# First layer's remaining modulation vectors: two weight blocks per visit, loaded into the softmax's wide tiles

## The chip, the cores and the metric

The kernel runs on one NeuronCore of a Trainium2 chip. A core has several engines with an instruction queue each: TensorE (PE) multiplies matrices, VectorE (DVE) and ScalarE (ACT) work elementwise, GpSimd (POOL) does a little of both, and SyncE (SP) issues the DMA transfers here. An engine runs its own queue in order and waits on semaphores for the others. The metric is the device time of one execution in microseconds (us), as the median of several runs.

## The reference

A transformer block of two layers, one sequence of 256 tokens (`x`) and a second stream of 256 context tokens (`ctx`), width 1024. Per layer, cut to what matters:

```python
mod = s_c @ w_mod[i] + b_mod[i]              # 6 vectors of 1024: sh1, sc1, gt1, sh2, sc2, gt2
mod_c = s_ctx @ w_mod[i] + b_mod[i]          # the same for the context (layer 1: two of them)
h = modulate(rms_norm(x, g_norm1[i]), sh1, sc1);  hc = the same of ctx
p = h @ w_in[i]                              # keys, queries, values, u, v, gate logits; pc from hc
y_na  = neighbourhood_attention(q_na, k_na, v_na, k_na_c, v_na_c, rpb)   # 8 heads of 64
y_gm  = spatial_gating(gelu(u), gelu(v), ...)
y_mla = dense_attention(q_mla, [k_mla_c, k_mla], [v_mla_c, v_mla])       # 8 heads of 96
mix = merge_branches(y_na, y_gm, y_mla, gates, na_w_o, gm_w_o, mla_w_o, w_out)
x = x + gt1 * mix
x = x + gt2 * squared_relu_mlp(modulate(rms_norm(x), sh2, sc2), w1, w2)
```

In layer 0 the context passes through all of this as well; in layer 1 it only gives keys and values. So layer 0 works on 512 columns (both streams) and layer 1 on 256. The shift and scale `sh1`, `sc1` are needed before anything else; the other four vectors (`gt1`, `sh2`, `sc2`, `gt2`) only after `merge_branches`. These four are the "other modulation vectors" of the title.

## The kernel before, in words

Activations stand transposed: 128 features on the partitions, tokens in the columns. Projections run in the precision of fp32 by splitting each operand in a rounded high part and the rest and adding three multiplications, high by high, high by low and low by high (`mm3`; lines 287, 288 and 289 of the profile). ScalarE makes the high part of a weight block (`wh`, line 115) and VectorE the rest (`wl`, line 116). `gemm_a` projects one chunk of 128 output features: 8 blocks of input features, so 24 multiplications of 512 columns in layer 0.

Weights come through `load` (line 94): a DMA of 512 KB (128 x 1024 fp32) from SyncE's queue into the ring `raw` of three buffers. `last_load` remembers the latest one; `tc.issue_after` orders other transfers behind it.

The order of the work on each engine is set when the program is built: the tile framework takes the operations of all parts and orders them by a simulated time line, within what data, buffers, priorities and `issue_after` allow. On the chip each engine then runs its list in order. So a small edit can move many instructions.

Layer 0 around the change runs like this: projections, then `u` (the loop at line 708, four chunks), the gating step `sg`, the neighbourhood attention (two heads at a time through `soft_pv`), the keys and values of the second attention (`kv`, with the transposes `h_tr`), its queries (`qm`), the second attention (`soft_pv` again, outputs `pvm`), and the merges. `merge(l, b, ...)` computes for branch b the gate logits (`gate`) and the branch's output projection (`z`), chunk by chunk. Multiplications of a merge are spread beside an attention by `paced`: `marks` holds the score multiplications, and each block of a gate or of `z` is released behind one of them. Branch 0 (gating) has its first four chunks beside the neighbourhood attention and the other four between the two attentions; branch 1 and the first gates of branch 2 go beside the second attention; the rest of branch 2 follows unpaced.

`soft_pv` (line 429) does a pair of heads and one stream: the score `S`, its maximum and the exponential `P` (ScalarE, line 448), four transposes `pt` (line 454) into one PSUM buffer, a copy by ScalarE to `PT` (line 456), and the product with the values (`pv`, `pvm`, line 460). `PT` is a wide tile, 128 x 1024 fp32 like a weight block, with two buffers, one for each head of the pair. The FFN's `load(..., extra=True)` uses the same two buffers under the name `rawx`.

The other modulation vectors are made by four generators `mod_group` (line 168), g = 2 to 5, each over the eight 128 x 1024 blocks of its part of `wmod`. Each step of a generator is a *visit*: `load` one block into `raw`, then `mod_cols`, four multiplications of a 128 x 32 operand by 256 columns each (the silu of both conditions, of which two columns hold data), and `yield`. The trace shows a visit as eight records of `mod_ps`, line 137. `bg()` (line 122) takes one step of the first generator that isn't through. It is called in the `u` loop (`bg(2)`, line 710) and in each chunk of each merge (line 478). After the eighth block `mod_finish` copies the sums to `mod_sb`, transposes them (`mod_t`) and adds the bias.

Of the kernel before, what the change touches and what calls it, by code (L numbers as in the profile page):

```python
# [7 lines left out]
F32 = mybir.dt.float32  # L8
# [15 lines left out]
KC = 8  # L24


def hybrid_block_kernel(tc, a, out):
    nc = tc.nc
    act = nc.scalar.activation
    vec = nc.vector  # L30
    mm = nc.tensor.matmul

    from contextlib import ExitStack, nullcontext
    with ExitStack() as es:
# [7 lines left out]
        gp = pool("g")  # L42
# [40 lines left out]
        sS = cp.tile([128, KC, 32], F32, name="sS")  # L83
# [12 lines left out]
        last_load = [None]  # L96

        def load(ap, width=1024, extra=False):
            if extra:
                raw = gp.tile([128, 1024], F32, tag="PT", name="rawx", bufs=2)  # L100
            else:
                raw = wp.tile([128, 1024], F32, tag="raw", name="raw", bufs=3)
            dma = nc.sync.dma_start(out=raw[:, :width], in_=ap)
            if not extra:
                last_load[0] = dma.ins
            return raw
# [15 lines left out]
        def bg(n=1):  # L122
            while n and background:
                try:
                    next(background[0])
                    n -= 1
                except StopIteration:
                    background.pop(0)
# [5 lines left out]
        def mod_cols(ps, raw, off, w, k):  # L134
            for j in range(4):
                o = off + j * w
                mm(ps[32 * j:32 * j + 32, :w], lhsT=sS[:, k, :], rhs=raw[:, o:o + w], start=(k == 0), stop=(k == KC - 1),
                   tile_position=(0, 32 * j))

        def mod_finish(ps, w, dsts, modT, bmod, streams):  # L140

# [25 lines left out]

        def mod_group(l, g, modT, bmod, streams):
            ps = psum("mm", "mod_ps")
            for k in range(KC):  # L170
                raw = load(a["wmod"][l, g - 2, k])
                mod_cols(ps, raw, 0, 256, k)
                yield
            mod_finish(ps, 256, lambda m, i: m[:, 8 * g:8 * g + 8].rearrange("p (j i) -> p j i", i=2)[:, :, i], modT, bmod,
                       streams)

# [297 lines left out]
        def merge(l, b, yH, yL, hH, hL, ymix, T, ns=range(8), pace=None, gated={}):  # L474

            mixH, mixL = [], []
            for n in ns:
                bg()
                if n in gated:
                    th = gated[n]  # L480
                    if n % 2 == 0:
                        zraw = load(a["wo"][l, b, n // 2])
                else:
                    gw = split(load(a["wa"][l, 4 + 8 * b + n]))
                    if n % 2 == 0:
                        zraw = load(a["wo"][l, b, n // 2])
                    gps = psum("mm", "gate")
                    gemm_a(gps, gw, hH, hL, T, pace=pace)
                    th = tmp2("th")
                    act(out=th[:, :T], in_=gps[:, :T], func=AF.Tanh, scale=0.5)  # L490
                zps = psum("mm", "z")
                gemm_a(zps, [split1(zraw[:, (n % 2) * 512:(n % 2) * 512 + 512], 512)], yH, yL, T, pace=pace)
                if b == 0:
                    o = xp.tile([128, NT], F32, tag="ymix", name="ymix", bufs=8)
                    vec.scalar_tensor_tensor(out=o[:, :T], in0=th[:, :T], scalar=1.0, in1=zps[:, :T], op0=ALU.add,
                                             op1=ALU.mult)
                    ymix.append(o)
                else:
                    o = ymix[n]
                    vec.scalar_tensor_tensor(out=th[:, :T], in0=th[:, :T], scalar=1.0, in1=zps[:, :T], op0=ALU.add,  # L500
                                             op1=ALU.mult)
                    vec.tensor_tensor(out=o[:, :T], in0=o[:, :T], in1=th[:, :T], op=ALU.add)
                if b == 2:
                    H, Lo = parts("mix", T)
                    act(out=H[:, :T], in_=o[:, :T], func=AF.Copy, scale=0.5)
                    vec.scalar_tensor_tensor(out=Lo[:, :T], in0=o[:, :T], scalar=0.5, in1=H[:, :T], op0=ALU.mult,
                                             op1=ALU.subtract)
                    mixH.append(H)
                    mixL.append(Lo)
            return mixH, mixL  # L510
# [17 lines left out]
        first, rest = begin_mod(0)  # L528
# [18 lines left out]
        for l in range(L):  # L547
# [22 lines left out]
            with tc.issue_after(last_load[0]):  # L570
                if l == 0:
# [8 lines left out]
                                  in_=a["kqrow"][l:l + 1, :].to_broadcast([128, 64]))  # L580
# [20 lines left out]
            for w in range(2):  # L601
                for t in range(2):
                    vec.tensor_tensor(out=rC[:, w, t, :], in0=ropeC[:, t, :], in1=kqrow[:, w, :], op=ALU.mult)
                    for hf in range(2):
                        o = rS[:, w, t, :].rearrange("p (a b f) -> p a b f", a=2, b=2)[:, :, hf, :]
# [19 lines left out]
            for t in range(4):  # L625
                o = gp.tile([128, 512], F32, tag="v", name="vna", bufs=4)
# [83 lines left out]
                                  op1=ALU.mult)  # L710
            u = []
            for n in range(4):
                bg(2)
                ws = split(load(a["wa"][l, n]))
                ups = psum("mm", "u")
                gemm_a(ups, ws, hH, hL, T)
                o = g2("u", F32)
                act(out=o[:, :T], in_=ups[:, :T], func=AF.Gelu)
                u.append(o)
# [350 lines left out]
```

## Time and profile before

| | |
|---|---|
| median of 3 runs | 1403.13 us (1402.51 to 1403.38) |
| the profiled execution's own time | 1402.83 us |
| its span, first to last instruction | 1400.8 us |
| TensorE busy | 1370.2 us (98%) |
| VectorE, ScalarE, GpSimd busy | 957.4 (68%), 704.7 (50%), 56.9 us (4%) |
| chain that ended last | TensorE 96%, VectorE, DMA and ScalarE 1% each |

The span is what the page's parts divide; the execution's own time has 2.0 us more around it. Busy time of TensorE is modelled for pipelined multiplications: one that is shown as 0.39 us may be followed by the next 0.22 us after its start, so steps are read from start to start, and an idle time in square brackets is what the engine stood still before a row. The name behind the arrow in the brackets is what ended the wait.

### The profile page before, as it was taken

What the parts mean: (1) busy time and instruction counts of PE and PEld (TensorE: products, weight loads), DVE (VectorE), ACT (ScalarE), POOL (GpSimd) and SP (SyncE); (2) the same over time, 40 slices, a digit from 0 to 9 for tenths busy, and PEclk for the clock granted to TensorE, in tenths of its full rate; (3) what the DMA queues carried; (4) which work ended last, traced back from release to release, by engine and by line L of the source; (5) the groups of instructions that cost most, each with busy time, mean ns of one, the idle gap of its engine ahead of it and who ended that gap; (6) DMA issues with size and microseconds to landing.
All of it is one profiled execution on the core that took longest, in us unless ns stands there. A gap on an engine that the chain in (4) does not pass through costs nothing.

```text
span 1400.8 us, 22572 instructions
## 1 busy us (share of the span) xinstructions
PE 1370.2 (98%) x8438; PEld 1161.8 (83%) x8438; DVE 957.4 (68%) x2071; ACT 704.7 (50%) x1440; POOL 56.9 (4%) x35
## 2 busy tenths in 40 slices
PE   6999999999999999999999999999999999999999
PEld 4788767777676789988888888988888878999998
DVE  4666477665563558899766665786787766877775
ACT  3466256443453346623324233566676665656654
POOL 0110000110000000000000000011002100000000
PEclk9999999999999999999999999999999999999999
DMA  9423542234313465665555552443543434566664
GB/s 331 142 84 106 187 150 90 71 105 123 119 46 114 127 195 168 208 202 172 203 205 188 175 197 89 150 137 94 181 136 99 136 91 136 181 181 180 183 183 148
DMA packets 67214, 210.61 MB, mean 150 GB/s; under 512 B 8609, under 2 KB 9633, under 8 KB 67105
## 3 DMA queue, kind: packets, MB, share of 16 engines
q1 hardware_dynamic: 67104, 209.18, 46.6%
q8 instruction: 66, 1.08, 0.3%
q14 instruction: 44, 0.35, 0.1%
HBM read 208.10 MB, written 1.05 MB: 149 GB/s over the span
## 4 chain that ended last, share of the span: by engine, by line
PE 96%; DVE 1%; DMA 1%; ACT 1%; issue 0%; SPq 0%; POOL 0%; ACTq 0%; DVEq 0%
PE o_ps L287 8%; PE o_ps L289 8%; PE o_ps L288 8%; PE f L288 6%; PE f L287 6%; PE f L289 6%; PE gate L287 5%; PE gate L288 5%; PE gate L289 5%; PE b_ps L287 5%; PE b_ps L288 4%; PE b_ps L289 4%; PE pt L454 3%; PE S L417 2%; PE z L287 2%; PE z L289 2%
## 5 line engine op out<-in xcount | busy, mean ns | idle before, releaser
L115 ACT ACTIVATE wh<-raw 128x512 fp32r<-128x512 f32 (+1 forms) x570 | 353.1, 626 | 515.8 <-PE o_ps L288 179.7
L116 DVE TENSOR_TENSOR wl<-raw,wh 128x512 fp32r<-128x512 f32 (+1 forms) x570 | 385.8, 683 | 178.1 <-ACT wh L115 172.7
L289 PE MATMUL f<-hH,wl 128*128 128x258 f32 (+2 forms) x560 | 180.9, 324 | 0.1
L287 PE MATMUL f<-hH,wh 128*128 128x258 f32 (+2 forms) x560 | 180.4, 323 | 0.5 <-ACT wh L115 0.5
L288 PE MATMUL f<-hL,wh 128*128 128x258 f32 (+2 forms) x560 | 180.4, 324 | 0.2 <-DVE hL L277 0.2
L288 PE MATMUL o_ps<-aL,wh 128*128 128x256 f32 (+1 forms) x544 | 176.1, 327 | 0.0
L287 PE MATMUL o_ps<-aH,wh 128*128 128x256 f32 (+1 forms) x544 | 176.0, 328 | 0.0
L289 PE MATMUL o_ps<-aH,wl 128*128 128x256 f32 (+1 forms) x544 | 175.6, 328 | 0.0
L287 PE MATMUL gate<-hH,wh 128*128 128x512 f32 (+1 forms) x384 | 140.5, 366 | 0.0
L289 PE MATMUL gate<-hH,wl 128*128 128x512 f32 (+1 forms) x384 | 130.3, 339 | 0.0
L288 PE MATMUL gate<-hL,wh 128*128 128x512 f32 (+1 forms) x384 | 130.1, 339 | 0.0
L287 PEld LDWEIGHTS f<-hH,wh 128*128 128x128 f32 x560 | 106.0, 190 | 9.1 <-ACT wh L115 0.7
L289 PEld LDWEIGHTS f<-hH,wl 128*128 128x128 f32 x560 | 106.2, 190 | 8.5 <-DVE wl L116 0.3
L288 PEld LDWEIGHTS f<-hL,wh 128*128 128x128 f32 x560 | 105.9, 190 | 8.5 <-DVE hL L277 0.4
L287 PEld LDWEIGHTS o_ps<-aH,wh 128*128 128x128 f32 x544 | 102.7, 190 | 9.5 <-ACT aH L937 0.8
L288 PEld LDWEIGHTS o_ps<-aL,wh 128*128 128x128 f32 x544 | 103.1, 190 | 8.5
L289 PEld LDWEIGHTS o_ps<-aH,wl 128*128 128x128 f32 x544 | 102.7, 190 | 8.8
L288 PE MATMUL b_ps<-wl,hH 128*128 128x512 f32 (+2 forms) x288 | 108.8, 381 | 0.0
L289 PE MATMUL b_ps<-wh,hL 128*128 128x512 f32 (+2 forms) x288 | 106.3, 381 | 0.0
L287 PE MATMUL b_ps<-wh,hH 128*128 128x512 f32 (+2 forms) x288 | 103.7, 385 | 0.0
L200 DVE SCALAR_TENSOR_TENSOR macc<-rawx,sS,macc 128x512 f32<-128x512 f32 x112 | 78.9, 748 | 32.7 <-DMA rawx<-in_wmod_dram 32.4
L287 PEld LDWEIGHTS gate<-hH,wh 128*128 128x128 f32 x384 | 72.7, 189 | 15.9 <-issue 7.5
(229 smaller groups left out, 2481.3 us busy)
## 6 DMA issues: line engine op xcount, KB each, us to landing
raw<-in_wa_dram SPq DMA_DIRECT2D x147, 512.0 KB, 3.6
raw<-in_w_dram SPq DMA_DIRECT2D x68, 512.0 KB, 3.6
raw<-in_wb_dram SPq DMA_DIRECT2D x32, 512.0 KB, 3.3
raw<-in_wmod_dram SPq DMA_DIRECT2D x32, 512.0 KB, 3.4
rawx<-in_wmod_dram SPq DMA_DIRECT2D x32, 512.0 KB, 4.5
raw<-in_wo_dram SPq DMA_DIRECT2D x24, 512.0 KB, 3.6
rawm<-in_wmod_dram SPq DMA_DIRECT2D x32, 256.0 KB, 6.0
rawx<-in_wmod_dram SPq DMA_DIRECT2D x32, 256.0 KB, 4.2
```

What stands on the lines that cost most here:

```text
L115: act(out=wh[:, :width], in_=src, func=AF.Copy)
L116: vec.tensor_tensor(out=wl[:, :width], in0=src, in1=wh[:, :width], op=ALU.subtract)
L200: summed = vec.scalar_tensor_tensor(out=o, in0=src, scalar=s, in1=o, op0=ALU.mult, op1=ALU.add)
L287: mm(ps, lhsT=sh, rhs=mh, start=first, stop=False)
L288: mm(ps, lhsT=sh, rhs=ml, start=False, stop=False)
L289: mm(ps, lhsT=sl, rhs=mh, start=False, stop=last)
L417: return mm(s, lhsT=Q[h][0:96, q0:q0 + 128], rhs=K[h][0:96, k0:k0 + nk], start=True, stop=True)
L454: nc.tensor.transpose(pt[:, i * 128:(i + 1) * 128], P[:, i * 128:(i + 1) * 128], ident)
```

## The change

`mod_group` takes the blocks in pairs. A step begins by loading a pair into two wide tiles of tag `PT` (named `rawx`), the tiles in which the softmax keeps its transposed weights, ordered behind the last ring load; then it yields, and the multiplications of the pair stand at the beginning of the next step. The first of them waits for both transfers (the added dependency). `mod_cols` returns its first multiplication for that. In a merge `bg()` is called only where the merge is not paced, so not beside the attentions, and the `u` loop takes one step instead of two. There are 16 visits of two blocks in place of 32 of one: four in the `u` loop, four in the second half of branch 0 between the attentions, eight in branch 2.

```diff
--- before.py
+++ after.py
@@ -134,8 +134,10 @@
         def mod_cols(ps, raw, off, w, k):
             for j in range(4):
                 o = off + j * w
-                mm(ps[32 * j:32 * j + 32, :w], lhsT=sS[:, k, :], rhs=raw[:, o:o + w], start=(k == 0), stop=(k == KC - 1),
-                   tile_position=(0, 32 * j))
+                m = mm(ps[32 * j:32 * j + 32, :w], lhsT=sS[:, k, :], rhs=raw[:, o:o + w], start=(k == 0),
+                       stop=(k == KC - 1), tile_position=(0, 32 * j))
+                first = m if j == 0 else first
+            return first
 
         def mod_finish(ps, w, dsts, modT, bmod, streams):
 
@@ -167,10 +169,18 @@
 
         def mod_group(l, g, modT, bmod, streams):
             ps = psum("mm", "mod_ps")
-            for k in range(KC):
-                raw = load(a["wmod"][l, g - 2, k])
-                mod_cols(ps, raw, 0, 256, k)
+            for kp in range(KC // 2):
+                with tc.issue_after(last_load[0]):
+                    raws = [gp.tile([128, 1024], F32, tag="PT", name="rawx", bufs=2) for _ in range(2)]
+                    for i in range(2):
+                        dma = nc.sync.dma_start(out=raws[i], in_=a["wmod"][l, g - 2, 2 * kp + i])
                 yield
+
+                for i in range(2):
+                    m = mod_cols(ps, raws[i], 0, 256, 2 * kp + i)
+                    if i == 0:
+                        tc.add_manual_dep(m.ins, dma.ins.name, mybir.DependencyInfo(
+                            mybir.DependencyClass.Sync, mybir.DependencyReason.DATA), reason="both blocks")
             mod_finish(ps, 256, lambda m, i: m[:, 8 * g:8 * g + 8].rearrange("p (j i) -> p j i", i=2)[:, :, i], modT, bmod,
                        streams)
 
@@ -475,7 +485,8 @@
 
             mixH, mixL = [], []
             for n in ns:
-                bg()
+                if pace is None:
+                    bg()
                 if n in gated:
                     th = gated[n]
                     if n % 2 == 0:
@@ -710,7 +721,7 @@
                                   op1=ALU.mult)
             u = []
             for n in range(4):
-                bg(2)
+                bg()
                 ws = split(load(a["wa"][l, n]))
                 ups = psum("mm", "u")
                 gemm_a(ups, ws, hH, hL, T)
```

Only layer 0 has this work, and only between its first `u` chunk and its output projection does any engine's list differ. The lines behind the edit shift by ten (297 to 299 are 287 to 289 of before, 464 and 470 are 454 and 460). What moved, in three places:

TensorE at the first half of layer 0's neighbourhood attention, of before and of the change (`S` are scores, `gate` is branch 0's gate projection, `pt` the transposes of the softmax weights `P`, `mod_ps` a visit; `naQL` is the low part of the queries):

```order
L287 MATMUL gate<-hH,wh 128x512
L288 MATMUL gate<-hL,wh 128x512
L289 MATMUL gate<-hH,wl 128x512
L454 MATMUL pt<-ident,P 128x128 x4
L137 MATMUL mod_ps<-raw,sS 32x256 x4
L454 MATMUL pt<-ident,P 128x128 x4
L410 MATMUL S<-naK,naQ 128x256
L411 MATMUL S<-naK,naQL 128x256
L287 MATMUL gate<-hH,wh 128x512
```

```order
L297 MATMUL gate<-hH,wh 128x512
L298 MATMUL gate<-hL,wh 128x512
L299 MATMUL gate<-hH,wl 128x512
L464 MATMUL pt<-ident,P 128x128 x8
L420 MATMUL S<-naK,naQ 128x256
L421 MATMUL S<-naK,naQL 128x256
L297 MATMUL gate<-hH,wh 128x512
L298 MATMUL gate<-hL,wh 128x512
L299 MATMUL gate<-hH,wl 128x512
```

The block between the first two groups of transposes is gone, and the two groups stand side by side.

TensorE at the end of layer 0's second attention, of before (`pvm` is the last product with the values, `z` with `yml` is the projection of its result, `gate` belongs to later chunks):

```order
L288 MATMUL gate<-hL,wh 128x512
L289 MATMUL gate<-hH,wl 128x512
L287 MATMUL gate<-hH,wh 128x512
L460 MATMUL pvm<-PT,vml 64x256 x4
L288 MATMUL gate<-hL,wh 128x512
L289 MATMUL gate<-hH,wl 128x512
L287 MATMUL gate<-hH,wh 128x512
L288 MATMUL gate<-hL,wh 128x512
L289 MATMUL gate<-hH,wl 128x512
L137 MATMUL mod_ps<-raw,sS 32x256 x4
L287 MATMUL z<-yml,wh 128x512 x2
L288 MATMUL z<-yml,wh 128x512
```

and of the change (`mod_t` are the transposes of the third group's sums, `rawx` the first pair of the fourth):

```order
L297 MATMUL z<-yml,wh 128x512
L298 MATMUL z<-yml,wh 128x512
L299 MATMUL z<-yml,wl 128x512
L464 MATMUL pt<-ident,P 128x128 x2
L148 MATMUL mod_t<-ident,mod_sb 128x128 x2
L464 MATMUL pt<-ident,P 128x128 x4
L470 MATMUL pvm<-PT,vml 64x256 x4
L297 MATMUL z<-yml,wh 128x512
L298 MATMUL z<-yml,wh 128x512
L299 MATMUL z<-yml,wl 128x512
L137 MATMUL mod_ps<-rawx,sS 32x256 x8
L297 MATMUL gate<-hH,wh 128x512
```

Before, the last `pvm` has gate rows on both sides. Now `z` rows, transposes, `pvm`, three `z` rows and the pair follow each other, and the gate comes behind the pair.

SyncE's queue there, of before (`in_wa` are gate blocks, `in_wo` blocks of the branches' output projections, `in_wmod` the modulation's blocks):

```order
L103 DMA raw<-in_wa_dram 128x1024
L103 DMA raw<-in_wo_dram 128x1024
L103 DMA raw<-in_wmod_dram 128x1024
L103 DMA raw<-in_wa_dram 128x1024
L103 DMA raw<-in_wmod_dram 128x1024
L103 DMA raw<-in_wa_dram 128x1024
L103 DMA raw<-in_wo_dram 128x1024
L103 DMA raw<-in_wmod_dram 128x1024
```

and of the change:

```order
L103 DMA raw<-in_wa_dram 128x1024 x2
L103 DMA raw<-in_wo_dram 128x1024
L103 DMA raw<-in_wa_dram 128x1024
L176 DMA rawx<-in_wmod_dram 128x1024 x4
L103 DMA raw<-in_wa_dram 128x1024
L176 DMA rawx<-in_wmod_dram 128x1024 x2
L103 DMA raw<-in_wo_dram 128x1024
L103 DMA raw<-in_wa_dram 128x1024
L176 DMA rawx<-in_wmod_dram 128x1024 x2
```

The modulation blocks stood one by one between ring loads. Now four of them stand together (two pairs, one behind the other in the two `PT` buffers), and beside the attention the ring carries only `wa` and `wo`.

## Rows read from the trace of the kernel before

**Rows 1.** The page's first lines: span, busy time and share of each engine.

```profile
span 1400.8 us, 22572 instructions
PE 1370.2 (98%) x8438; PEld 1161.8 (83%) x8438; DVE 957.4 (68%) x2071; ACT 704.7 (50%) x1440; POOL 56.9 (4%) x35
```

**Rows 2.** Busy by stretch: length, PE, PEld, DVE, ACT, POOL, PEclk, DMA, GB/s.

```profile
180.00:260.00 80.00, 76.95 (x452) 53.76 (x451) 60.44 (x158) 52.77 (x133) 3.63 (x2) 1.00 0.30 98
260.00:332.00 72.00, 70.00 (x371) 56.37 (x370) 41.22 (x86) 29.11 (x61) 10.02 (x6) 1.00 0.37 109
332.00:455.00 123.00, 122.68 (x647) 85.80 (x646) 63.08 (x150) 56.21 (x135) 0.00 (x0) 1.00 0.30 96
```

**Rows 3.** TensorE's timeline: start, duration, operation; visits among projection rows.

```profile
318.32 0.39 PE L288 MATMUL z<-yna,wh 128*128 128x512 f32 x1
318.54 0.39 PE L289 MATMUL z<-yna,wl 128*128 128x512 f32 x1
318.86 0.64 PE L137 MATMUL mod_ps<-raw,sS 128*32 128x256 f32 x8
319.43 0.50 PE L287 MATMUL gate<-hH,wh 128*128 128x512 f32 x1
...
353.25 1.07 PE L137 MATMUL mod_ps<-raw,sS 128*32 128x256 f32 x16
354.25 0.66 PE L454 MATMUL pt<-ident,P 128*128 128x128 f32 x4
```

**Rows 4.** TensorE's timeline, rows with idle time before them in brackets.

```profile
187.29 0.50 PE L410 MATMUL S<-naK,naQ 128*128 128x512 f32 x1 [0.29 <-ACT P L448]
...
191.33 0.64 PE L137 MATMUL mod_ps<-raw,sS 128*32 128x256 f32 x8 [1.04 <-DMA raw<-in_wmod_dram]
...
209.44 0.66 PE L454 MATMUL pt<-ident,P 128*128 128x128 f32 x4 [0.75 <-ACT PT L456]
...
289.62 0.64 PE L794 MATMUL h_tr<-ident,knat 128*96 128x128 f32 x4 [1.75 <-DVE kml L798]
290.51 0.45 PE L287 MATMUL qm<-wh,cq 128*128 128x384 f32 x1 [0.25 <-ACT qnat L817]
290.79 0.34 PE L288 MATMUL qm<-wl,cq 128*128 128x384 f32 x1
290.97 0.35 PE L289 MATMUL qm<-wh,cq 128*128 128x384 f32 x1
```

**Rows 5.** SyncE's timeline, two loads issued together, and when both landed.

```profile
143.98 0.33 SPq L103 DMA_DIRECT2D raw<-in_wmod_dram  x1
144.41 0.37 SPq L103 DMA_DIRECT2D raw<-in_wa_dram  x1
...
DMA to landing us min/median/max: 3.3/3.7/4.1
```

**Rows 6.** TensorE's timeline, end of layer 1's second attention.

```profile
1158.01 0.66 PE L454 MATMUL pt<-ident,P 128*128 128x128 f32 x4 [0.75 <-ACT PT L456]
...
1159.56 0.63 PE L454 MATMUL pt<-ident,P 128*128 128x128 f32 x4 [0.89 <-DVE P L451]
...
1160.87 1.95 PE L460 MATMUL pvm<-PT,vml 128*64 128x256 f32 x16 [0.69 <-ACT PT L456]
...
1163.30 0.66 PE L287 MATMUL z<-yml,wh 128*128 128x256 f32 x2 [0.48 <-ACT yml L423]
```

**Rows 7.** TensorE's timeline, end of layer 0's second attention.

```profile
449.83 1.08 PE L460 MATMUL pvm<-PT,vml 128*64 128x256 f32 x8
450.84 0.51 PE L288 MATMUL gate<-hL,wh 128*128 128x512 f32 x1
```

**Rows 8.** The stretch after the first data, by windows and on TensorE's timeline.

```profile
11.90:26.00 14.10, 13.54 (x125) 8.78 (x129) 9.16 (x30) 5.96 (x14) 1.65 (x2) 1.00 1.01 367
...
24.82 0.63 PE L287 MATMUL b_ps<-wh,hH 128*128 128x512 f32 x1
25.25 0.63 PE L288 MATMUL b_ps<-wl,hH 128*128 128x512 f32 x1
```


## The prediction

> **What bounds the kernel now.** I read the page first, then the busy times by stage, then TensorE's timeline where it idles. The page says that TensorE is busy 1370.2 of 1400.8 us [rows 1]. So only two things can move the time: what TensorE executes, and its idle stretches. The change touches layer 0 from the first `u` projection to the output projection, about 143 to 501 us. Outside it the order of every engine is the same. By stage [rows 2], TensorE idles 3.05 us during the neighbourhood attention (180 to 260 us), 2.00 us while the keys and queries of the second attention are made (260 to 332 us) and 0.32 us in that attention (332 to 455 us). That is 5.4 us in all, so there is little to win. A second attention with two streams of tokens and next to no idle time is a thing that can only get worse. The reader should see in the waits [rows 4] that each one has one instruction behind it.
>
> **The sum** is made against the profiled execution's own 1402.83 us, that is its span of 1400.8 and 2.0 around it; the median of the runs shown, 1403.13, is 0.3 above it.
>
> **1. Fewer, longer visits.** The 128 matrix multiplications for the 32 weight blocks stay (four to a block; the trace has two records for each). What goes is changeovers. A visit of one block between two projections takes from 318.86 to 319.43, 0.57 us, one of two blocks from 353.25 to 354.25, 1.00 us [rows 3]. In the order of before the blocks stand in 32 runs: 23 single blocks, three doubles, and three blocks cut in two. Counting a piece like a single that is 23 x 0.57 + 3 x 1.00 + 6 x 0.57 = 19.5 us. In the order of the change they stand in 19 runs: 14 whole pairs, and two pairs cut into five pieces (one of 5 multiplications, one of 7, between the two rows 0.68 and 0.89, and three of 1 or 2, each again 0.57): 17.3 us. That saves 2.2 us. Going in and out costs more: the block at 318.86 starts 0.32 us after the row before, where projection rows follow each other after 0.22 (318.32 to 318.54), so 0.1, and about as much on the way out. With 13 runs fewer that is 0 to 2.6 us. Many of the lost runs stood beside transposes or scores, which pay for the changeover anyway, so I take 0.6. Together **-2.8** (bounds -2.2 and -4.8).
>
> **2. The neighbourhood attention.** The four blocks of its first half go, and with them the wait for a block at 191.33 (1.04) and the wait of a score at 187.29 (0.29) [rows 4]. But the block stood between two groups of transposes `pt`, which share one PSUM buffer: the second waits until ScalarE has copied the first. The order of the change puts them side by side. Such neighbours cost 0.75 at 209.44 [rows 4]. One more pair of neighbours arises in the third pair of heads, 0.75 again. The third score now follows the gating step with fewer projection rows between; it needs the first exponential, behind the same VectorE work as before, so its wait grows: I take one more 0.75 (bounds 0.3 and 2.5). At the end a wait of 0.3 for the keys falls away, as projections now stand there. Together -1.33 - 0.3 + 3 x 0.75 = **+0.6** (bounds -1.3 and +2.7).
>
> **3. Keys and queries, 260 to 332 us.** Three groups of key transposes stood too close and waited 1.75 and then 0.25 us for VectorE's and ScalarE's copies [rows 4]. In the new order a block of six `qm` rows or the pair itself stands between them: **-2.0** (bounds -2.0 and 0). The third pair of group 3 is issued when the second is through and used after 18 `qm` rows of 0.18 and 8 transposes [rows 4], some 4.2 us later. Of two loads issued together the second landed 0.43 + 4.1 = 4.5 us after the first's issue [rows 5]. With 0.3 for the hand-over to the queue and back I count 4.8 - 4.2 = **+0.6** (bounds 0 and 1.5). Here the load is hidden by nothing else.
>
> **4. The middle of the second attention.** The last pair of group 3 was loaded before it and is worked off inside it: seven of its eight multiplications stand after some 17 projection rows that follow the first `pt`. Until then both softmax tiles are taken and the copy of that `pt` waits, and ScalarE's queue behind it (exponentials and weight splits). Projection rows cover this on TensorE. But then two `pt` groups are neighbours, and at the second pair of heads `pvm` follows its last `pt` directly; layer 1's end shows 0.69 for that [rows 6]. Together **+1.5** (bounds 0 and 2.2).
>
> **5. The end of the second attention.** This term decides. In before the last `pvm` stands between gate projections and nothing waits (449.83 and 450.84) [rows 7], as the blocks' order let the gates of two further chunks in ahead of it. In the order of the change there are eight `z` rows behind the last score, then the last transposes, `pvm`, three more `z` rows that need its result, and then the first pair of group 4. No gate stands among them. Layer 1 ends in just this way, without cover: 0.75, 0.89, 0.69 and 0.48 us of waits, 2.8 us [rows 6]. Layer 0's copies after `pvm` are twice as wide, so I take 3.3.
>
> Then comes the pair. Its two loads go into the softmax tiles that this `pvm` reads last, so they are issued only when it ends, at the head of SP's queue. They are there 4.8 us later (term 3's count), and TensorE, whose rows run in order, has only three `z` rows to do, which wait about 1.0 us for the copies of `pvm`'s result (the 0.48 and the half for the width) and take 0.7. It then stands for 4.8 - 1.7 = 3.1 us. What queues behind the pair on TensorE is the gate of chunk 1 and all that follows. Behind the loads on SP stand only weights needed two chunks later, so no second wait. Before, a 0.32 us wait [rows 2] stood here, which goes. Together 3.3 + 3.1 - 0.3 = **+6.1** (bounds +3 and +8).
>
> What such gaps do to the clock can be read from the steps of the rows. Layer 1's end has four gaps within some 6 us, and its groups of four transposes still take 0.66 and 0.63 us [rows 6], as one in full flow (354.25) [rows 3]. Behind the longest gap after the first data, 1.75 us, `qm` rows of 384 columns stand 0.18 us apart [rows 4], near the 0.16 of 2.4 GHz and far from the 0.32 of 1.2 GHz. "TensorE: Matmul & The Clock Gate" of the Trainium skill (Part 1: The HAM clock gate) says that the array falls back to half its clock once it has sat idle, and needs sustained work to come back; by that rule the new stall would cost more than its own length, and the sum would be that of the third rival. Gaps up to 1.75 us have not done it here; 3 us no row shows.
>
> **6. The other visits.** In the last merge each pair is loaded when the one before is through and used 36 projection rows later, 36 x 0.22 = 7.9 us against 4.8: hidden, 0. The same holds for the three pairs in the `u` projections (35 rows between). The weight ring loses 32 loads, but no wait for a ring load of projection weights stands in these stages, so 0. If that cover went, each late pair would cost up to 4.8 us.
>
> **Sum:** -2.8 + 0.6 - 2.0 + 0.6 + 1.5 + 6.1 = +4.0 us, or 1406.8 in the profiled execution's count and **1407.1 us** against the median. About 0.2% (2.8 us) is what a measurement here can tell from no change, so the forecast lies on the slower side, by 1.2 us.
>
> **Rivals.**
> First, gains and losses cancel. If the neighbours of terms 2 and 4 cost nothing, because a chain that is late anyway takes them in, the sum is +4.0 - 1.5 - 1.5 = +1.0: 1404.1 us. For it speaks that such waits overlap; against it that the 0.75 at 209.44 was not taken in.
> Second, faster: the end of the second attention stays covered. If the last softmax ends while TensorE still works on the eight `z` rows and the two loads land while it waits for `pvm`'s copies, term 5 is about +0.3; with the neighbours taken in as well the sum is -2.8 - 0.9 - 2.0 + 0.6 + 0.3 = -4.8: 1398.3 us. It decides from the point where the loads could start before `pvm` ends. Against it: they go into tiles that `pvm` reads.
> Third, the clock: after a stall of some 3 us TensorE falls to its lower level, 1.2 GHz, and climbs back as at the start. There, after the wait for the first data, rows of 512 columns stood 0.43 us apart (24.82 to 25.25) instead of 0.22, though the granted clock of that stretch reads 1.00 [rows 8]. If all its 14.1 us ran so, half of them were lost, 7 us: 1414.1 us. Against it: the 1.75 us gap. This is the rule above, from the Trainium skill.
> Fourth, the change does not free the attention: the pair that is held inside the second attention (term 4) keeps ScalarE's queue closed for so long that weight splits come late. The queue is closed for the 17 projection rows, 17 x 0.22 = 3.7 us, and if TensorE feels all of it, the time is 1410.8 us. Against it: the weight splits run a step ahead.
>
> **How the numbers follow.** Forecast 0.57, cancelling 0.27, faster 0.08, clock 0.04, closed queue 0.04. Of the forecast's share 0.08 lies below the 0.2% line, since its sum is only 1.2 above it. So slower 0.49 + 0.08 = 0.57, same 0.27 + 0.08 = 0.35, faster 0.08. The likeliest case alone lies between 1404.5 and 1410. The range for 8 in 10 takes in most of cancelling and the closed queue: 1402.8 to 1411.0.
>
> **What would show it.** In the profile after: runs of 16 multiplications of about 1.00 us (term 1); no wait of `mod_ps` for a load in the neighbourhood attention, and two more waits of `pt` for ScalarE's copy (2); no 1.75 us before `h_tr` (3); a wait of `pvm` for its copy (4); at the end of the second attention four waits as in layer 1, and then the longest wait of all after the first data, some 3.1 us, of `mod_ps` for `rawx` (5). The prediction is wrong if that last wait is under 1 us, or if gates still run between the last transposes and `pvm`; it is wrong the other way if `mod_ps` waits for `rawx` in the last merge too, or if the granted clock falls.

## The result and the profile after

The changed kernel takes 1412.28 us (median of 6 runs, 1410.33 to 1412.89) against 1402.81 us for the kernel before (6 runs, 1402.2 to 1403.38). The ratio is 1.0067, with a 95% interval of 1.0057 to 1.0076: 9.5 us slower. The prediction said 1407.1, between 1402.8 and 1411.0. The direction was right, the size was missed, and the time lies above the range. Of all executions reported here one, of zlast3, took 4793.03 us; it is left out of that run's ratio.

The head of the page after, with TensorE's row of the slices, answers to [rows 1]:

```profile
span 1410.3 us, 22597 instructions
PE 1372.7 (97%) x8438; PEld 1165.9 (83%) x8438; DVE 957.4 (68%) x2071; ACT 707.3 (50%) x1440; POOL 57.4 (4%) x35
...
PE   6999989999998999999999999999999999999999
...
PEclk9999999999998999999999999999999999999999
```

TensorE runs as many multiplications as before, is busy 2.5 us longer, and the span is 9.5 us longer. One slice of the clock's row (the thirteenth, 423 to 458 us) is an 8 where before all forty were 9. The windows show it better (columns as in [rows 2]; the granted clock is the third figure from the end):

```profile
180.00:260.00 80.00, 73.88 (x406) 53.63 (x405) 58.84 (x151) 50.94 (x130) 3.30 (x2) 0.98 0.23 71
260.00:332.00 72.00, 71.50 (x384) 57.49 (x383) 39.69 (x89) 30.11 (x62) 10.80 (x6) 1.00 0.38 123
332.00:455.00 123.00, 117.15 (x587) 82.53 (x586) 63.70 (x147) 55.46 (x133) 0.00 (x0) 0.96 0.23 73
185.00:189.00 4.00, 3.69 (x10) 2.93 (x11) 2.44 (x7) 0.93 (x4) 0.00 (x0) 0.57 0.17 58
434.00:445.00 11.00, 7.93 (x33) 4.00 (x34) 3.28 (x5) 1.98 (x4) 0.00 (x0) 0.53 0.48 180
```

TensorE now idles 6.1 us in the first stretch and 5.9 in the third, and in two short stretches, 185 to 189 and 434 to 445 us, the clock is granted at little more than half: 1.2 GHz for most of them. The first is behind one wait in the neighbourhood attention (TensorE's timeline):

```profile
182.34 0.39 PE L299 MATMUL z<-yg,wl 128*128 128x512 f32 x1
185.31 0.80 PE L420 MATMUL S<-naK,naQ 128*128 128x512 f32 x1 [2.58 <-ACT P L458]
185.90 0.63 PE L421 MATMUL S<-naK,naQL 128*128 128x512 f32 x1
186.33 0.63 PE L297 MATMUL gate<-hH,wh 128*128 128x512 f32 x1
...
190.50 0.66 PE L464 MATMUL pt<-ident,P 128*128 128x128 f32 x4 [0.69 <-ACT PT L466]
```

The third score waits 2.58 us for an exponential, where before it waited 0.29 [rows 4], and the rows behind it stand 0.43 us apart instead of 0.23. The second is the end of the second attention:

```profile
432.04 0.44 PE L464 MATMUL pt<-ident,P 128*128 128x128 f32 x2 [0.32 <-ACT PT L466]
433.26 0.44 PE L464 MATMUL pt<-ident,P 128*128 128x128 f32 x2 [0.78 <-ACT PT L466]
434.17 1.85 PE L470 MATMUL pvm<-PT,vml 128*64 128x256 f32 x8 [0.47 <-ACT PT L466]
436.73 0.80 PE L297 MATMUL z<-yml,wh 128*128 128x512 f32 x1 [0.72 <-ACT yml L433]
437.46 0.80 PE L298 MATMUL z<-yml,wh 128*128 128x512 f32 x1
438.05 0.63 PE L299 MATMUL z<-yml,wl 128*128 128x512 f32 x1
440.86 1.93 PE L137 MATMUL mod_ps<-rawx,sS 128*32 128x256 f32 x16 [2.18 <-DMA rawx<-in_wmod_dram]
```

Here stand the four waits and the stall that the prediction named. But `pvm` already takes 1.85 us where it took 1.08 [rows 7]: the clock had fallen before the long stall, after 1.57 us of waits in the 2.5 us ahead of it. It came back at about 444.5, so all that TensorE did in between ran at half speed. SyncE's row shows why the pair is late:

```profile
436.12 7.06 SPq L176 DMA_DIRECT2D rawx<-in_wmod_dram  x4
```

The first load starts when `pvm` has just ended (434.17 + 1.85 = 436.02), and `mod_ps` starts 4.7 us after the load's start.

**The ledger.** The time up to the first `u` row differs from one execution to the next (over all kernels run here that row stands between 139.94 and 144.28 us). So the stage is taken from the first `u` row to the first row of the output projection: 144.28 to 500.82 before, 142.28 to 509.76 after, 356.54 and 367.48 us, 10.9 more. Its waits over 20 ns sum to 5.35 before and 12.39 after, +7.0. The half clock costs about 1.5 in the neighbourhood attention (0.59 and six times 0.43 from row to row, instead of 0.34 and 0.23) and about 3.2 at the end of the second (`pvm` 0.8, `z` 0.7, the pair 0.9, gate rows 0.8), +4.7. The visits, from start to start without waits, took 18.5 us for 30 blocks before (two more stood ahead of the stage) and 17.6 for 32 after, the half clock taken out: 0.62 and 0.55 each, so -2.1 for 32, and +1.2 for the two that came into the stage. Sum 7.0 + 4.7 - 2.1 + 1.2 = 10.8 of the 10.9.

### The profile page after: what moved, and what is told of

Its sections match the earlier page's. It is cut to its first block, busy times and chain, and to the rows that moved or that the text cites. A ratio compares the mean times of both kernels' runs of the same rounds, so it can differ in the third digit from the quotient of the medians.

```text
span 1410.3 us, 22597 instructions
## 1 busy us (share of the span) xinstructions
PE 1372.7 (97%) x8438; PEld 1165.9 (83%) x8438; DVE 957.4 (68%) x2071; ACT 707.3 (50%) x1440; POOL 57.4 (4%) x35
## 3 DMA queue, kind: packets, MB, share of 16 engines
q8 instruction: 66, 1.08, 0.3%
## 4 chain that ended last, share of the span: by engine, by line
PE 96%; ACT 1%; DMA 1%; DVE 1%; issue 0%; SPq 0%; POOL 0%; ACTq 0%; DVEq 0%
PE o_ps L297 8%; PE o_ps L299 8%; PE o_ps L298 8%; PE f L298 6%; PE f L299 6%; PE f L297 6%; PE gate L297 5%; PE gate L298 5%; PE gate L299 5%; PE b_ps L297 4%; PE b_ps L298 4%; PE b_ps L299 4%; PE pt L464 3%; PE S L427 2%; PE z L297 2%; PE z L298 2%
```

## Experiments

Two places had to be told apart (the neighbourhood attention, the end of the second attention), and three causes: missing cover, the sharing of the softmax tiles, and the clock. Each run has 4 to 11 executions. "Before" below is the kernel before on the same chip: 1402.04 us for place, tailring, nacover and fillna, 1401.68 for nahold, gatefirst, zlast3 and nazl3, 1401.98 for exporder, expzl3 and nacz. Since the kernel before itself differs by up to 1.1 us from chip to chip (1402.81 beside the change), a difference between two runs below can be off by about as much.

**place**: the kernel before with other places alone, no shared tiles.

```diff
             for n in ns:
-                bg()
+                if pace is None:
+                    bg(2)
```

> The kernel before with only the place of the visits changed: single blocks in the weight ring as before, but none beside an attention; the u loop and the unpaced merge steps take two each. Its TensorE order in the neighbourhood attention is nearly that of the change; at the end of the second attention 24 gate rows and a visit stand between the last transposes. Theory (the loss is two uncovered stretches, each with a fall of the clock): the long wait of the third score (2 us or more) and a stretch of half clock stay in the neighbourhood attention, the end of the second attention has no wait above 0.8 us and no fall; 1406 us (1404.5 to 1408). Rival (the sharing of the softmax tiles costs it, not the place): nothing is shared here, so as before, 1402.8 us.

Measured 1425.51 us, ratio 1.0170 (1.0152 to 1.0187). Both expectations fell. The third score waits 1.35 us with no half clock behind it, the end of the attention keeps waits of 0.48, 0.47 and 0.93, and most is lost in the last merge (TensorE's timeline):

```profile
463.00 0.79 PE L287 MATMUL gate<-hH,wh 128*128 128x512 f32 x1 [3.96 <-ACT wh L115]
488.83 0.79 PE L287 MATMUL gate<-hH,wh 128*128 128x512 f32 x1 [4.03 <-ACT wh L115]
513.45 0.79 PE L287 MATMUL gate<-hH,wh 128*128 128x512 f32 x1 [3.89 <-ACT wh L115]
```

The gate waits for the high part of its own weights (`wh`), and ScalarE, which makes it, waits for their load (ScalarE's timeline):

```profile
462.32 1.67 ACT L115 ACTIVATE wh<-raw 128x512 fp32r<-128x512 f32 x3 [2.09 <-DMA raw<-in_wa_dram]
```

So three buffers do not carry two blocks a step beside gates and `z`, and each of these waits has half clock behind it. With the visits at these places the shared tiles are no cost but a gain: the change, which has them, is 13 us faster.

**tailring**: in the change, the first visit of the last merge goes through the ring.

```diff
+                if ring[0]:
+                    for i in range(ring[0]):
+                        mod_cols(ps, load(a["wmod"][l, g - 2, k]), 0, 256, k)
+                        k += 1
+                    yield
+                    continue
...
                 if pace is None:
+                    ring[0] = 2 if (b, n) == (2, 0) else 0
                     bg()
+                    ring[0] = 0
```

> The changed kernel with one visit changed: the visit in the first step of the last merge takes its two blocks through the weight ring and multiplies at once; the other visits as in the change. Theory: the neighbourhood attention keeps its 2.58 us wait and half clock, the 2.18 us stall of mod_ps and the waits at the last softmax go, and the clock stays at 2.4 GHz there: 1412.3 - 4.2 - 3.5 = 1404.6 us (1403.5 to 1406.5). Rival (only the stall itself matters; the clock falls from the softmax waits all the same): 1412.3 - 2.2 = 1410.1 us.

Measured 1411.99 us, 1.0071 (1.0057 to 1.0084): nothing won, and both expectations missed. The waits at the end of the attention are gone, all but 0.31, and the clock stays up there. But the new order puts two later pairs next to each other (472.49 and 478.20 us), and the second waits for its load, again with half clock behind it (TensorE):

```profile
478.20 1.94 PE L138 MATMUL mod_ps<-rawx,sS 128*32 128x256 f32 x16 [3.59 <-DMA rawx<-in_wmod_dram]
```

**nacover**: the same switch, but for one block a step beside the neighbourhood attention.

```diff
-                if pace is None:
+                if pace is None or b == 0:
+                    ring[0] = 1 if pace is not None else 0
                     bg()
+                    ring[0] = 0
```

> The changed kernel, but the four steps of the first merge beside the neighbourhood attention take one block each again, through the weight ring; all other visits are pairs in the softmax tiles. TensorE's order has blocks between the second and third score and between the first transposes again, and, by the scheduler, 24 gate rows at the end of the second attention. Theory: both uncovered stretches go, no fall of the clock: 1412.3 - 4.2 - 7.7 = 1400.4 us (1399 to 1403). Rival (sharing the tiles costs it): pairs still share them in 14 visits, so no lower than 1407 us.

Measured 1416.08 us, 1.0100 (1.0084 to 1.0115). In the neighbourhood attention the expectation held: no wait of a score, full clock. Behind the second attention three pairs now follow each other (the first at 450.48 us), and the second and third are late (TensorE):

```profile
457.33 1.93 PE L138 MATMUL mod_ps<-rawx,sS 128*32 128x256 f32 x16 [5.78 <-DMA rawx<-in_wmod_dram]
...
463.88 1.94 PE L138 MATMUL mod_ps<-rawx,sS 128*32 128x256 f32 x16 [3.40 <-DMA rawx<-in_wmod_dram]
```

So wherever the scheduler sets a pair less than a load's time behind the one before, it stands.

**fillna**: nine multiplications whose result nobody reads, ahead of the first wait (`fill` holds their operands, for the first pair of heads of layer 0 alone).

```diff
+                    if fill and (v, qt) == (0, 1):
+                        with tc.issue_after(marks[-1]):
+                            for _ in range(9):
+                                mm(pv, lhsT=fill[0], rhs=fill[1], start=True, stop=True)
```

> The changed kernel with nine multiplications of 512 columns added whose result is overwritten, on TensorE right behind the second score of the neighbourhood attention; every other row stands as in the change. They take 2.05 us. Theory A (the wait of the third score is a chain from the second score over VectorE and the exponential, whatever TensorE does meanwhile): they fill the wait, 2.58 falls to about 0.5, the clock stays up: 1412.3 - 1.6 = 1410.7 us. Theory B (ScalarE's exponential, with its table load, stands behind a weight split that waits for the last z row before the wait, so rows put ahead of that z push the chain back): the wait stays 2.5 us, the clock falls as before, and the time is 1412.3 + 2.05 = 1414.3 us.

Measured 1408.35 us, 1.0047 (1.0033 to 1.0061): with 2.05 us of added work it is faster than the changed kernel, by 3.9 us from median to median and by 2.8 from ratio to ratio. The wait is gone altogether (TensorE):

```profile
179.85 2.23 PE L447 MATMUL pv<-hH 128*128 128x512 f32 x9
...
183.74 0.39 PE L299 MATMUL z<-yg,wl 128*128 128x512 f32 x1
183.97 0.39 PE L420 MATMUL S<-naK,naQ 128*128 128x512 f32 x1
```

That is more than theory A gave. In the profile the stage is 3.3 us shorter than in the change (364.21 and 367.48). About 2.0 of that stand here: 2.58 of waiting and 1.5 of half clock less, 2.05 of rows more. About 1.1 stand at the end of the second attention, which the edit leaves alone: there `pvm` took 1.08 us behind the same three waits, at full clock. And ScalarE shows why even the 2.0 are not the nine rows' own: its order had changed. In the change a weight split stands ahead of the exponentials and waits for a `z` row, and the table load waits behind it (ScalarE's timeline of the changed kernel):

```profile
180.49 0.60 ACT L501 ACTIVATE th<-gate 128x512 f32<-128x512 f32 x1
182.54 0.63 ACT L115 ACTIVATE wh<-raw 128x512 fp32r<-128x512 f32 x1 [1.45 <-PE z L298]
183.18 1.28 ACT L458 ACT_TABLE_LOAD   x1
184.48 0.69 ACT L458 ACTIVATE P<-S,nm 128x512 f32<-128x512 f32 x1
```

With the nine rows the scheduler had set that split behind the exponentials. So the edit had cut B's chain, and could not tell A from B. The next run does.

**exporder**: on ScalarE only that split moved (on VectorE its low part and one softmax scaling change places with it); TensorE's order is the same row for row.

```diff
+                        if len(exps) < 2:
+                            exps.append(done.ins)
...
+                    raw = load(a["wa"][l, 4 + 8 * b + n])
+                    with tc.issue_after(exps[1]) if (l, b, n) == (0, 0, 2) else nullcontext():
+                        gw = split(raw)
```

> The changed kernel with one instruction moved: on ScalarE the weight split that stands ahead of the first exponentials of the neighbourhood attention (and there waits for a z row) is held behind them. TensorE's order is the same row for row. Theory (that place on ScalarE's queue makes the wait of the third score): the table load starts right behind the gate's tanh, some 2 us earlier, and the 2.58 us wait falls to some 0.5; with no half clock behind it 1412.3 - 2.1 - 1.5 = 1408.7 us, with the half clock still there 1410.2 us. Rival (the wait comes from VectorE's chain for the row maximum, or from too few rows on TensorE): the wait stays above 1.5 us, 1411 us or more.

(`done` is the exponential.) Measured 1408.25 us, 1.0039 (1.0025 to 1.0053), as expected. ScalarE's timeline, then TensorE's at the third score:

```profile
178.15 0.60 ACT L507 ACTIVATE th<-gate 128x512 f32<-128x512 f32 x1
178.77 1.28 ACT L460 ACT_TABLE_LOAD   x1
180.06 0.69 ACT L460 ACTIVATE P<-S,nm 128x512 f32<-128x512 f32 x1
```

```profile
180.89 0.50 PE L420 MATMUL S<-naK,naQ 128*128 128x512 f32 x1 [0.51 <-ACT P L460]
```

The place of one split on ScalarE made 2.07 of the 2.58 us, and the half clock there (1.5) with it. In the profile the stage is 3.4 us shorter than in the change (364.10 us), from median to median it is 4.0. The kernel is as fast as fillna without the nine rows, so those paid nothing themselves.

**nahold**: the last pair of the `u` loop behind the second score.

```diff
+                    with tc.issue_after(hold[0]) if (g, kp) == (2, 3) else nullcontext():
+                        m = mod_cols(ps, raws[i], 0, 256, 2 * kp + i)
...
+            hold[0] = marks[1]
```

> The changed kernel with one pair moved: the last pair of the u loop multiplies behind the second score of the neighbourhood attention instead of ahead of the first. Nothing is added; on ScalarE the exponential and its table load now stand ahead of the weight split that waits for a z row (in the change they stand behind it). Theory (that order on ScalarE makes the 2.58 us wait, and the wait makes the half clock there): the wait of the third score falls to some 0.4 us, no half clock at about 185 us: 1412.3 - 2.2 - 1.5 = 1408.6 us (1407.5 to 1410). Rival (TensorE simply lacks rows there: one pair more gives its 1.0 us and what lay ahead of the first score loses it): the wait falls to about 1.5 us, the attention starts 1 us earlier, the clock falls or not: 1411 us or more.

Measured 1408.28 us, 1.0051 (1.0037 to 1.0065). The time is the theory's, its wait is not: 1.65 us stayed, and in the profiled execution the half clock too (it is the slowest of the four, 1410.42 us; the others took 1407.29 to 1408.31). The split does stand behind the exponentials here. But other rows moved with the pair. Two `z` rows slipped behind the third score, so that TensorE, counted from the gating's last rows, reaches it 0.5 us earlier than in exporder. And ScalarE's tanh, with the table load behind it, waits 0.63 us for VectorE, which now works on the scores first; the exponential comes 0.66 later. With the 0.51 of exporder that is the 1.65.

**gatefirst**: the visits of the last merge behind the gate of their step.

```diff
-                if pace is None:
+                if pace is None and not (b == 2):
                     bg()
...
                     gemm_a(gps, gw, hH, hL, T, pace=pace)
+                    if pace is None and (b == 2):
+                        bg()
```

> The changed kernel with the visits of the last merge called behind the gate projection of their step instead of ahead of it. TensorE's order at the end of the second attention then has 24 gate rows between the last transposes, but the first pair of the fourth group still stands three z rows behind the last pvm. So the softmax waits (0.32, 0.78, 0.47 us) go and the stall for the pair stays, 2.2 to 2.7 us. Theory A (the stall alone is enough for the clock to fall): half clock for some 4 us behind it, as in the run with nine added rows: 1412.3 - 1.6 - 2 = 1408.7 us. Theory B (the fall needs the softmax waits ahead of it): no half clock at all there: 1412.3 - 1.6 - 3.5 = 1407.2 us.

Measured 1413.45 us, 1.0082 (1.0068 to 1.0096). Its premise failed: the gate rows came ahead of the next to last transposes, and the last ones still waited (TensorE):

```profile
439.85 0.44 PE L464 MATMUL pt<-ident,P 128*128 128x128 f32 x2 [1.08 <-ACT PT L466]
440.76 1.08 PE L470 MATMUL pvm<-PT,vml 128*64 128x256 f32 x8 [0.47 <-ACT PT L466]
442.56 0.49 PE L297 MATMUL z<-yml,wh 128*128 128x512 f32 x1 [0.72 <-ACT yml L433]
...
447.12 1.94 PE L137 MATMUL mod_ps<-rawx,sS 128*32 128x256 f32 x16 [3.10 <-DMA rawx<-in_wmod_dram]
```

It doesn't tell theory A from B. It does show the stall behind rows at full clock, 3.10 us (in fillna 2.73) beside the 3.1 predicted: in the change the slowed `z` rows had eaten a part of it.

**zlast3**: the visits of the last merge at the end of their step, held behind its `z` rows, none in the second and third step.

```diff
-                if pace is None:
+                if pace is None and b != 2:
                     bg()
...
+                if b == 2 and pace is None and n not in (1, 2):
+                    after[0] = lastmm[0]
+                    bg()
+                    after[0] = None
```

(`after[0]` goes to `tc.issue_after` around the pair's multiplications.)

> The changed kernel with the visits of the last merge at the end of their step, held behind its z rows, and none in its second and third step: between the last pvm and the first pair stand some 47 gate and z rows, 10 us, and gate rows between the last transposes. Two visits move behind the merge. Theory (the end of the second attention costs 4.2 us of waits and 3.5 of half clock, and both come from missing cover): no wait above 0.8 us there and no half clock: 1412.3 - 4.2 - 3.5 = 1404.6 us (1403.5 to 1406). Rival (what is freed is given back later, as a pair that is late in the output projection or as another fall of the clock): 1407 us or more.

Measured 1404.64 us, 1.0016 (1.0005 to 1.0027), as expected. The end of the attention keeps one wait, the pair has none, and both run at full clock (TensorE):

```profile
445.48 1.08 PE L474 MATMUL pvm<-PT,vml 128*64 128x256 f32 x8
447.28 0.97 PE L301 MATMUL z<-yml,wh 128*128 128x512 f32 x3 [0.72 <-ACT yml L437]
...
457.92 1.07 PE L137 MATMUL mod_ps<-rawx,sS 128*32 128x256 f32 x16
```

**nazl3**, **expzl3** and **nacz** put the repairs together: zlast3 with nahold, with exporder, and with nacover's single blocks.

> Both repairs together: the last pair of the u loop behind the second score, and the visits of the last merge at the end of their step, none in its second and third. Theory: both losses go, and what is left of the change is its gain from fewer visits and the keys: 1412.3 - 3.7 - 7.7 = 1400.9 us (1399.5 to 1402), below the kernel before (1402.8). Rival (the losses overlap or move): 1403 us or more.

> The moved weight split (exponentials first) together with the pairs of the last merge at the end of their step: the two repairs without any other change of the visits' places. Theory: waits of about 6.6 us, no half clock: 1404.6 - 2.1 - 1.0 = 1401.5 us, the same as before within the noise. Rival: half clock or a wait stays, 1403.5 us or more.

> Single blocks through the weight ring beside the neighbourhood attention (as in the run with that edit alone, which waited only 0.34 us there), and in the last merge the pairs at the end of their step, held behind its z rows and left out in the second and third. Theory: no wait above 0.8 us between the first score and the output projection and no half clock; waits sum to some 5.6 us against 5.2 before, visits save about 2.5: 1400 us (1398.5 to 1401.5) against 1401.7 to 1402.8 before. Rival (pairs in the softmax tiles are late again somewhere): 1403 us or more.

Measured 1401.60 (0.9996, 0.9987 to 1.0006), 1403.14 (1.0000, 0.9991 to 1.0009) and 1402.51 us (0.9996, 0.9985 to 1.0006). All three are the same as before within the measurement; the loss is gone, and none of the three gains anything, so nothing was found that beats the kernel before. In the profiles of nazl3 and expzl3 the longer visits save about 1.7 us, and the waits of the stage are 2.4 and 1.2 us above before. For nacz 1400 us was expected, with 2.5 saved by the visits. Its waits came as expected, 5.7 us, but its 30 blocks in the stage stand in 22 pieces, where before they stood in 31, and save only 0.4.

## Why the prediction was wrong, step by step

- **1, visits.** -2.8 was forecast, -2.1 measured. The shorter rows (-2.2) came. The 0.6 for going in and out lies outside this count, from start to start; the ledger closes to 0.1 us without it.
- **2, neighbourhood attention.** +0.6 was forecast, +3.0 measured in waits (6.05 after, 3.02 before) and 1.5 in clock. The neighbours came as said (0.69 and a second 0.75 new). The 0.3 for the keys did not go: `pv` and `kv` wait 0.77 and 0.51 us there, where 0.52 and 0.32 stood. The mis-sized term is the third score: "I take one more 0.75 (bounds 0.3 and 2.5)", measured 2.58 against 0.29, +2.29. I counted rows on TensorE and looked at VectorE's queue, and left ScalarE's out: a split had moved ahead of the table load. The order of the change on ScalarE showed it, and exporder measured it, 2.07 us.
- **3, keys and queries.** -2.0 and +0.6 forecast; -1.5 measured (2.00 to 0.50). The pair that was to be late there was not.
- **4, middle of the second attention.** +1.5 forecast, 0.69 and 0.69 measured.
- **5, its end.** +6.1 forecast, +4.2 measured in waits: 2.29 in the softmax (3.3 forecast) and 2.18 for the pair (3.1 forecast, and 2.73 and 3.10 in fillna and gatefirst, where the clock stayed up until the pair), less 0.32. The mechanism was right, and removing it (zlast3) gave 7.6 us back from median to median, the half clock there with it.
- **The clock** is the step that failed. The sum gave it nothing, and it took 4.7 us: 1.5 behind the third score, 3.2 at the end of the second attention. Some of that would else have been waiting, since the load was on its way while the slowed `z` rows ran: in fillna and gatefirst, behind a `pvm` at full clock, TensorE stood 2.95 and 3.33 us from the first of these `z` rows to the pair (0.22 and 0.23 for the rest of `pvm`'s result, then for the load), instead of 2.18. So without the half clock the changed kernel would by the ledger have been at about 1408.5 (an estimate), 1.4 above the forecast and inside the range. The mis-sized wait of step 2 is a part of this, as 1.5 of the 4.7 stand behind it: exporder, which takes away that wait and its half clock, lies at 1408.25, inside the range too. The third rival told of this cost, at 7 us and behind a stall of 3 us alone; I gave it 4 in 100, with the sentence "Gaps up to 1.75 us have not done it here". That was read from one execution. Layer 1's end was my evidence [rows 6]. No kernel here changes it, its waits are the same in all 13 profiles (within 0.01 us), and in five of them (nacover, exporder, zlast3, expzl3, nacz) it runs into half clock. In nacz (TensorE's timeline):

```profile
1156.31 0.66 PE L479 MATMUL pt<-ident,P 128*128 128x128 f32 x4 [0.75 <-ACT PT L481]
1157.86 0.63 PE L479 MATMUL pt<-ident,P 128*128 128x128 f32 x4 [0.89 <-DVE P L476]
1159.17 3.27 PE L485 MATMUL pvm<-PT,vml 128*64 128x256 f32 x16 [0.69 <-ACT PT L481]
```

`pvm` takes 3.27 us there against 1.95 in [rows 6]. The other way round, the end of layer 0's second attention in exporder has the three waits of the change, and the clock is still up:

```profile
426.16 0.44 PE L468 MATMUL pt<-ident,P 128*128 128x128 f32 x2 [0.32 <-ACT PT L470]
427.38 0.44 PE L468 MATMUL pt<-ident,P 128*128 128x128 f32 x2 [0.78 <-ACT PT L470]
428.29 1.08 PE L474 MATMUL pvm<-PT,vml 128*64 128x256 f32 x8 [0.47 <-ACT PT L470]
```

`pvm` took 1.85 us there in the change. And nahold and nazl3 have the same wait before the third score. First nahold, then nazl3:

```profile
183.36 0.56 PE L422 MATMUL S<-naK,naQ 128*128 128x512 f32 x1 [1.65 <-ACT P L460]
183.72 0.63 PE L423 MATMUL S<-naK,naQL 128*128 128x512 f32 x1
```

```profile
185.14 0.50 PE L426 MATMUL S<-naK,naQ 128*128 128x512 f32 x1 [1.65 <-ACT P L464]
185.47 0.39 PE L427 MATMUL S<-naK,naQL 128*128 128x512 f32 x1
```

The second score row takes 0.63 us at half clock in the one and 0.39 in the other. "TensorE: Matmul & The Clock Gate" of the Trainium skill (Part 1: The HAM clock gate) says of the slow multiplications at a kernel's start that their number is "run-variable", since what the chip looks at runs free of the kernel. The rows here vary from execution to execution in the same way, and far from the start. The prediction weighed the page's rule without that sentence.

The rival "faster" was wrong on its point (the loads did wait for `pvm`), "closed queue" showed nowhere (no row of TensorE waits for a weight split in the changed kernel), and "cancelling" failed on the neighbours, whose new waits of 0.69, 0.75, 0.69 and 0.69 us stand in full. That sharing the tiles is itself the cost is refuted by place, which does not share them and is slower, and by nazl3 and expzl3, which do and are as fast as before. Which waits make the clock fall, and which don't, stays open. The profiles show half clock behind the 2.58 us wait in all four that have it (the change, tailring, gatefirst, zlast3), behind the 1.65 us wait in one of two, behind the waits of 0.32, 0.78 and 0.47 us in two of four (the change and nahold, not fillna and exporder), and at layer 1's end in five of 13.

## What to carry to other kernels

Small pieces of work that stand between dependent steps are cover; before they are moved, look at every engine's queue at the place they leave, above all at what now stands ahead of a table load and an exponential. A tile shared with a softmax can be filled only when its last reader is done, so its first use belongs a load's time and the hand-over behind that (here 4.6 to 6.2 us from the first load's start to the late pair's), and the order has to be forced, since the scheduler set pairs closer than that in most of the kernels run here. And where TensorE is busy 98% of the time, a wait is to be priced with the half clock that may follow it, from several executions and not from one.

## What the runs showed of the hardware that was not expected

- Work that nobody needs can seem to pay: the kernel with nine dead multiplications (2.05 us) was 3.9 us faster, but through the order on ScalarE that came with them; with that order alone, in exporder, it is as fast (1408.25 and 1408.35 us).
- The same rows with the same waits let the clock fall in one execution and not in another (`pvm` of layer 1's end 1.95 us in eight profiles, 3.27 to 3.55 in five).
- A change of ScalarE's table (1.28 us at 183.18) is started only when it heads the queue, so a split that waits ahead of it delays it in full. "ScalarE: Activation LUTs" of the Trainium skill (What ACT_TABLE_LOAD costs) gives about 1.28 us for the load, as here, and 1.38 more for a drain; here the exponential starts 0.02 us behind the load, and ScalarE's last work before it ends within 0.02 us of its start, so no drain shows.
